# Three raw weight buffers of 1024 words in place of two of 1120, in a fp32 transformer kernel

## The chip, the cores and the metric

The kernel runs on one core of a Trainium2 chip. The metric is the device time of one execution in microseconds (us); smaller is better. A kernel's figure is the median of several executions.

## The reference

The input is one sequence of 512 tokens with 1024 features in fp32, and 256 memory tokens. Two blocks follow each other. Cut to what matters here:

```python
def first_block(x, mem, ...):
    for i in range(2):
        ...
        x = x + jnp.concatenate([y_tok, y_mem], axis=-1) @ w_out
        h = rmsnorm(x, norm_ffn[i])
        x = x + (jax.nn.silu(h @ w_gate[i]) * (h @ w_up[i])) @ w_down[i]
    return rmsnorm(x, final_norm)

def compress_blocks(kv, pe, w1, w2):
    ...
    flat = blocks.transpose(0, 2, 1, 3).reshape(n_cmp, G, CMP_LEN * dh)
    return jax.nn.gelu(flat @ w1) @ w2

def second_block(x, ...):
        h = rms_norm(x, norm_pre)
        proj = h @ w_in
        (q_n, k_c, v_c, k_s, v_s, k_w, v_w, g_n, z_n,
         q_r, k_r, v_r, z_r, m_a, m_b) = jnp.split(proj, split_points(), axis=-1)
        ...
```

In the first block `y_tok` is a short convolution (layer 0) or a banded attention of 128 tokens (layer 1), `y_mem` an attention to the memory tokens. The second block has sparse attention (compressed keys, selected keys and a window, mixed by gates), a retention with four heads, and a gated merge. Hidden width of the feed-forwards is 2816.

## The kernel before

All activations stay in SBUF, features on partitions and 512 tokens along the free dimension, so a row of 1024 features is eight chunks of 128 x 512. Nearly all time is matmuls on PE, and each fp32 product is made of three: operands are split into a high part (a copy to float32r) and a low part (the rest), and high by high, high by low and low by high are added in PSUM. Tiles named ...h and ...l are such pairs.

Weights pass through `weights` (L103). It takes a raw tile `wr` of 1120 words a partition, tag wr with 2 buffers; SP issues the load (L111), ACT copies it to the high part `wh` (L70), and DVE subtracts to get the low part `wl` (L80). Tags wh and wl have 3 buffers each, so a weight's products must be done before the third weight after it can be split. Most weight units are 1024 words. The token-major projection of the values and gates (`w_in_vg`, here vg) is 8 x 280 columns in two units of four, which makes 1120 words; it is the only one over 1024. Its products (L142 to L144) go to four PSUM banks, one for each block of 128 tokens, tags pp and lg in turn, and each runs over eight chunks: four of the first unit, four of the second.

The feed-forwards (`ffn`, L651) have 22 hidden groups f of 128 x 2 features in bundles. The first 5 are plain, the other 17 are made by a Strassen-like scheme with 7 products in place of 8 (`gate_up`, L593). For each f, `pair_weights` (L562) takes **two** raw tiles (L569), copies and splits them into wh and wl (the parts a22 and a11), splits a12, and makes four sums s1 to s4 on DVE (L582), each split again on ACT and DVE. In `gate_up` a product is 12 matmuls (L603 to L605). One bank of tag pp, U, collects a11, s2, s3 and a22 one after the other, and ACT copies its partial states to g1, g2 and u in between; products a12, s1 and s4 go to other banks, and DVE adds them to g and u (L610). Products s1 and s4 share a bank, so the s4 product starts when DVE's add on u has read it; silu (L627) and two multiplications follow. Between the products, `between` puts down-projections of the bundle before.

In `second` (L956) the row R is spread over the partitions (`spread`, L198), the first key and the first value are projected and scaled by R, then two further keys (each scaled to a tile f, rotated in rb and ra, and split into stacks kh and kl), then vg, then a query, a gate, and the compression of k (`compress`, L809): flat tiles get an added position table pe (L823), are split, and meet four weight units of `cmp_w1` in 48 short matmuls (L832 to L834). The compression of v follows with further gates between, then the attention heads (`causal_head`, L923), which add the table `causal` to their logits. The causal table and the rows are constants with a place of their own; slots are tiles of 512 words by tag, with a number of buffers for each tag (s has 3, t 4, sa 1, k3 2, v3 1).

Each engine runs its instructions in the order in which they stand in its queue. That order is not the one of the code: the framework's scheduler makes it at build time, from what it takes each instruction to last and from when buffers of a tag come free. A change of buffers therefore moves instructions on all engines.

Of the kernel before, what the change touches and what calls it, by code (L numbers as in the profile page):

```python
# [8 lines left out]
F32 = mybir.dt.float32  # L9
# [19 lines left out]
class Build:  # L29
# [5 lines left out]
    def __init__(self, ctx, tc, T, out):  # L35
        self.tc, self.nc, self.T, self.out = tc, tc.nc, T, out
        pool = lambda n, b, **k: ctx.enter_context(tc.tile_pool(name=n, bufs=b, **k))
        self.cst = pool("cst", 1)
        self.wp = pool("wp", 1)
        self.wbufs = dict(wr=2, wh=3, wl=3)  # L40
        self.sl = pool("sl", 1)
        self.sm = pool("sm", 4)
        self.psp = pool("psp", 1, space=PSUM)
        self.dr = pool("dr", 1, space=DRAM)
        self.n = 0
        self.bufs = dict(h=8, b=16, t=4, pa=6, pb=10, q=4, v=4, x=8, R=1, s=3, sa=1, k3=2, v3=1)
        self.pbufs = dict(pp=2, lg=3, tp=2, po=1)
# [55 lines left out]
    def weights(self, src, nk, nn, parts=1):  # L103

        nc, n = self.nc, nk * nn
        raw = self.wp.tile([128, 1120], F32, name=self.nm("wr"), tag="wr", bufs=self.wbufs["wr"])
        hi = self.wp.tile([128, WMAX], F32R, name=self.nm("wh"), tag="wh", bufs=self.wbufs["wh"])
        lo = self.wp.tile([128, WMAX], F32R, name=self.nm("wl"), tag="wl", bufs=self.wbufs["wl"])
        step = n // parts
        for s in (slice(a, a + step) for a in range(0, n, step)):  # L110
            nc.sync.dma_start(raw[:, s], src[:, s] if parts > 1 else src)  # L111
        for s in (slice(a, a + step) for a in range(0, n, step)):
            self.copy(hi[:, s], raw[:, s])
            self.lo_of(lo[:, s], raw[:, s], hi[:, s])
        v = lambda t: t[:, :n].rearrange("p (k c) -> p k c", k=nk)
        return v(hi), v(lo)

# [80 lines left out]
    def spread(self, rs, name):  # L198

        nc, nt = self.nc, rs.shape[1]  # L200
        dg = self.slot("s", name="dg")
        for t in range(nt):
            nc.vector.tensor_scalar(dg[:, t * 128:t * 128 + 128], self.ident, rs[:, t:t + 1], None, op0=ALU.mult)
        ps = self.psum("tp")
        n = nt * 128
        nc.tensor.matmul(ps[:, :n], self.ones, dg[:, :n], start=True, stop=True)
        r = self.const(name, [128, n]) if n < 512 else self.slot("R", name=name)
        self.copy(r, ps[:, :n])
        return r

# [84 lines left out]
    def load_consts(self):  # L295
        nc, T = self.nc, self.T
        self.ident = self.const("ident", [128, 128])
        self.gains = self.const("gains", [128, 8 * 8])
        self.const("pad", [128, 88])
        self.ones = self.const("ones", [128, 128])  # L300
        nc.vector.memset(self.ones, 1.0)
        self.zero = self.const("zero", [128, 128], F32R)
        self.copy(self.zero, self.ones, 0.0)
        nc.scalar.dma_start(self.gains, T["gains"])
        nc.scalar.dma_start(self.ident, T["ident"])
        self.x = [self.slot("x", name="x") for _ in range(8)]
        nc.sync.dma_start(self.x[0], T["x"][:, 0])
        self.h0 = self.gained(self.x[:1], self.gain(0))
        self.w0 = [self.weights(T["a_w_in"][i], 8, 128, 2) for i in (0, 12)]
        for c in range(1, 8):  # L310
            nc.sync.dma_start(self.x[c], T["x"][:, c])
        self.conv = self.const("conv", [128, 18])
        nc.scalar.dma_start(self.conv, T["conv"])
        self.sink = self.const("sink", [128, 12])
        nc.scalar.dma_start(self.sink, T["b_sinks"].to_broadcast([128, 12]))
        self.negsink = self.const("negsink", [128, 12])
        nc.vector.tensor_scalar(self.negsink, self.sink, -1.0, None, op0=ALU.mult)
# [244 lines left out]
    def pair_weights(self, src):  # L562


        nc = self.nc
        k = lambda t: t.rearrange("p (k c) -> p k c", k=4)
        raw = [self.wp.tile([128, 1120], F32, name=self.nm("wr"), tag="wr", bufs=self.wbufs["wr"])[:, :1024] for _ in range(2)]
        for i, r in enumerate(raw):
            nc.sync.dma_start(r, src[:, 1024 * i:1024 * i + 1024])  # L569
        a22, a11, a12, a21 = (r[:, u:u + 512] for r in raw for u in (0, 512))  # L570
# [238 lines left out]
    def compress(self, kT, j):  # L809

        nc, T = self.nc, self.T
        pe = self.small(32)
        nc.gpsimd.dma_start(pe, T["cmp_pe"][j])
        fl = [self.slot("pb", name="flat")[:, :496].rearrange("p (l c) -> p l c", l=8) for _ in range(2)]
        for half in range(2):
            for par in range(2):
                for g in range(2):
                    src = kT[64 * g:64 * g + 64]
                    first = 16 * half + par
                    a = src[:, first:first + 1]  # L820
# [6 lines left out]
        for u in range(4):  # L827
            wh, wl = self.weights(T["cmp_w1"][j, u], 4, 256)
            for k in range(4):
                i = 4 * u + k  # L830
                a, b = (f[:, 62 * (i % 8):62 * (i % 8) + 62] for f in fs[i // 8])
# [124 lines left out]
    def second(self):  # L956
        nc, T = self.nc, self.T
# [12 lines left out]
        R = self.spread(rs, "R2")  # L970
# [2 lines left out]
        self.xd = self.dr.tile([8, 128, 512], F32, name="xraw")  # L973
        for c in range(8):
            nc.gpsimd.dma_start(self.xd[c], self.x[c])
        self.causal = self.const("causal", [128, 512])
        nc.gpsimd.dma_start(self.causal, T["causal"])
        self.cmask = self.const("cmask", [128, 128])
        nc.gpsimd.dma_start(self.cmask, T["cmask"])
# [340 lines left out]
```

## Time and profile before

| | |
|---|---|
| median of 3 runs | 1644.36 us (1644.22 to 1647.47) |
| profiled execution | 1646.98 us |
| its span in the trace | 1645.2 us |
| mean granted clock of PE in it | 0.996 |
| weight loads of the pairs (in_w_gu) | 68 of 512 KB, 3.9 us from issue to landing |
| weight loads of vg | 2 of 560 KB, 3.8 us |

The profiled execution is one run with its own time; the span is what the trace covers of it. Times of single instructions come from this execution. Engines are PE (matmul; PEld is its weight load), DVE (VectorE), ACT (ScalarE), POOL (GpSimd) and SP (which issues DMAs). A row of a timeline gives start, duration, engine, line, operation and the tiles, out<-in; in brackets is the idle time of that engine just before and what ended it. Instructions of PE overlap, so its pace is the distance between starts.

### The profile page before, as it was taken

The page shows a single profiled execution, that of the slowest core. Times are in us where ns is not written, and L with a number is a line of the kernel's source. Part 1 is how long each engine was busy: PE and PEld are TensorE (multiplying, and loading weights), DVE is VectorE, ACT ScalarE, POOL GpSimd, SP SyncE. Part 2 cuts the span into 40 slices and gives each one's busy share as a digit, 9 for nine tenths or more (in the row PEclk, how much of TensorE's full clock was granted, in tenths as well). Part 3 has the DMA queues.
Part 4 walks back from the last instruction along what each step waited for, and adds up shares of the span by engine and source line. Part 5 has one row for each costly group of instructions (what it writes and reads, how often), then busy time and mean ns, then how long its engine had stood idle before and what let it go on. Part 6 is the DMA issues. An engine that isn't in the chain of part 4 may idle for free.

```text
span 1645.2 us, 24463 instructions
## 1 busy us (share of the span) xinstructions
PE 1610.8 (98%) x9408; PEld 1408.5 (86%) x9408; DVE 1236.5 (75%) x2335; ACT 761.0 (46%) x1410; POOL 170.2 (10%) x179
## 2 busy tenths in 40 slices
PE   8999999999999999999999999998999999999998
PEld 6887888999999888888889999987888888888888
DVE  7876778777776889878777777698788877764444
ACT  6633344444444567625444444445465533333333
POOL 1112410000000300041000000111000000010011
PEclk9999999999999999999999999999999999999999
DMA  6227322333333623132332332343501122243342
GB/s 204 92 90 202 106 90 91 103 111 96 113 97 97 200 70 97 53 115 77 103 103 88 106 103 96 110 143 100 164 26 59 46 84 84 71 154 116 127 160 90
DMA packets 53877, 174.23 MB, mean 106 GB/s; under 512 B 6936, under 2 KB 9184, under 8 KB 53632
## 3 DMA queue, kind: packets, MB, share of 16 engines
q1 hardware_dynamic: 44928, 150.06, 28.0%
q0 software_dynamic: 8256, 22.49, 4.3%
q8 instruction: 74, 1.21, 0.3%
q14 instruction: 43, 0.35, 0.1%
q10 hardware_dynamic: 576, 0.11, 0.0%
HBM read 161.35 MB, written 13.65 MB: 106 GB/s over the span
## 4 chain that ended last, share of the span: by engine, by line
PE 75%; DVE 12%; DMA 6%; ACT 3%; issue 3%; POOL 1%; SPq 0%; DVEq 0%; ACTq 0%; POOLq 0%
PE pp L121 8%; PE pp L120 8%; PE pp L122 8%; DMA wr<-in_w_gu_dram 4%; PE lg L120 4%; PE lg L121 3%; PE lg L122 3%; DVE wl L80 3%; PE pp L603 3%; PE pp L604 3%; PE pp L605 3%; PE tp L120 3%; PE tp L121 3%; PE tp L122 3%; PE tp L262 2%
## 5 line engine op out<-in xcount | busy, mean ns | idle before, releaser
L70 ACT ACTIVATE wh<-wr 128x1024 fp32r<-128x1024 f32 (+3 forms) x246 | 252.0, 1024 | 344.8 <-PE pp L121 141.0
L80 DVE TENSOR_TENSOR wl<-wr,wh 128x1024 fp32r<-128x1024 f32 (+3 forms) x246 | 306.8, 1248 | 52.6 <-ACT wh L70 51.4
L120 PE MATMUL pp<-g,wh 128*128 128x512 f32 x592 | 235.0, 397 | 8.1 <-ACT wh L70 7.2
L122 PE MATMUL pp<-g,wl 128*128 128x512 f32 x592 | 234.4, 396 | 0.9 <-DVE wl L80 0.9
L121 PE MATMUL pp<-g,wh 128*128 128x512 f32 x592 | 233.1, 394 | 0.0
L120 PEld LDWEIGHTS pp<-g,wh 128*128 128x128 f32 x592 | 111.9, 189 | 31.0 <-ACT wh L70 8.2
L122 PEld LDWEIGHTS pp<-g,wl 128*128 128x128 f32 x592 | 111.6, 189 | 23.6 <-DVE wl L80 2.7
L121 PEld LDWEIGHTS pp<-g,wh 128*128 128x128 f32 x592 | 111.8, 189 | 20.3 <-DVE g L76 0.3
L70 ACT ACTIVATE s<-s 128x512 fp32r<-128x512 f32 x136 | 85.2, 631 | 52.1 <-DVE s L582 49.8
L120 PE MATMUL tp<-acth,wh 128*128 128x512 f32 x264 | 103.3, 391 | 0.0
L121 PE MATMUL tp<-actl,wh 128*128 128x512 f32 x264 | 103.3, 391 | 0.0
L122 PE MATMUL tp<-acth,wl 128*128 128x512 f32 x264 | 102.8, 389 | 0.0
L80 DVE TENSOR_TENSOR s<-s,s 128x512 fp32r<-128x512 f32 x136 | 90.3, 685 | 0.0
L603 PE MATMUL pp<-Bh,s 128*128 128x256 f32 x272 | 78.2, 288 | 3.3 <-ACT g L70 3.0
L582 DVE TENSOR_TENSOR s<-wr,wr 128x512 f32<-128x512 f32 x68 | 46.8, 689 | 44.6 <-DMA wr<-in_w_gu_dram 44.4
L603 PE MATMUL lg<-Bh,s 128*128 128x256 f32 x272 | 77.7, 286 | 0.8 <-DVE u L610 0.8
L605 PE MATMUL lg<-Bh,s 128*128 128x256 f32 x272 | 77.2, 284 | 0.0
L605 PE MATMUL pp<-Bh,s 128*128 128x256 f32 x272 | 76.9, 283 | 0.0
L248 POOL MEMSET v<- 128x1152 f32 x8 | 8.3, 1062 | 541.0 <-PE lg L605 541.0
L627 ACT ACTIVATE g<-g 128x512 f32<-128x512 f32 x34 | 21.5, 632 | 88.0 <-DVE g L610 88.0
L122 PEld LDWEIGHTS tp<-acth,wl 128*128 128x128 f32 x264 | 49.6, 188 | 10.9 <-DVE wl L80 0.3
L610 DVE TENSOR_TENSOR g<-lg,g 128x256 f32<-128x256 f32 x68 | 28.8, 423 | 38.8 <-PE lg L605 38.8
(512 smaller groups left out, 4611.5 us busy)
## 6 DMA issues: line engine op xcount, KB each, us to landing
wr<-in_w_gu_dram SPq DMA_DIRECT2D x68, 512.0 KB, 3.9
wr<-in_w_in_dram SPq DMA_DIRECT2D x44, 512.0 KB, 3.5
wr<-in_w_down_dram SPq DMA_DIRECT2D x32, 512.0 KB, 3.7
wr<-in_a_w_in_dram SPq DMA_DIRECT2D x18, 512.0 KB, 3.5
wr<-in_w_down_dram SPq DMA_DIRECT2D x16, 384.0 KB, 3.2
wr<-in_w_gate_dram SPq DMA_DIRECT2D x10, 512.0 KB, 3.5
wr<-in_w_up_dram SPq DMA_DIRECT2D x10, 512.0 KB, 3.5
wr<-in_a_w_out_dram SPq DMA_DIRECT2D x8, 512.0 KB, 3.5
```

The source lines that it names most:

```text
L70: self.nc.scalar.activation(out, in_, AF.Copy, scale=scale)
L80: self.nc.vector.tensor_tensor(out, x, hi.bitcast(F32), op=ALU.subtract)
L120: mm(ps, ah, bh, start=start, stop=False)
L121: mm(ps, ah, bl, start=False, stop=False)
L122: mm(ps, al, bh, start=False, stop=stop)
L262: self.nc.tensor.transpose(ps[:, c:c + 128], src, self.ident)
L582: nc.vector.tensor_tensor(t, a, b, op=ALU.add)
L603: mm(ps, ah, bh, start=start and j == 0, stop=False, skip_group_check=not start)
L604: mm(ps, ah, bl, start=False, stop=False, skip_group_check=not start)
L605: mm(ps, al, bh, start=False, stop=j == 3, skip_group_check=not start)
L610: add = lambda out, a, b: nc.vector.tensor_tensor(out, a, b, op=ALU.add)
L627: nc.scalar.activation(g, g, AF.Silu)
```

## The change

Raw tiles get three buffers of 1024 words in place of two of 1120. A vg unit is loaded in two pieces: 1024 words into the raw tile and 96 words into a slot of tag s, each with a load, a copy to the high part and a subtraction of its own. To make room, the causal table moves from a constant to a slot of tag sa, the memory row R of 256 tokens to a slot of tag v3, the position table of the compression to a slot of tag k3, and a padding constant shrinks from 88 words to 24.

```diff
-        self.wbufs = dict(wr=2, wh=3, wl=3)
+        self.wbufs = dict(wr=3, wh=3, wl=3)
...
-        raw = self.wp.tile([128, 1120], F32, name=self.nm("wr"), tag="wr", bufs=self.wbufs["wr"])
+        raw = self.wp.tile([128, 1024], F32, name=self.nm("wr"), tag="wr", bufs=self.wbufs["wr"])
...
-        step = n // parts
-        for s in (slice(a, a + step) for a in range(0, n, step)):
-            nc.sync.dma_start(raw[:, s], src[:, s] if parts > 1 else src)
-        for s in (slice(a, a + step) for a in range(0, n, step)):
-            self.copy(hi[:, s], raw[:, s])
-            self.lo_of(lo[:, s], raw[:, s], hi[:, s])
+        m = min(n, 1024)
+        step = m // parts
+        pieces = [(slice(a, a + step), raw[:, a:a + step]) for a in range(0, m, step)]
+        if n > m:
+            pieces.append((slice(m, n), self.slot("s", name="wr")[:, :n - m]))
+        for s, r in pieces:
+            nc.sync.dma_start(r, src if len(pieces) == 1 else src[:, s])
+        for s, r in pieces:
+            self.copy(hi[:, s], r)
+            self.lo_of(lo[:, s], r, hi[:, s])
...
-        r = self.const(name, [128, n]) if n < 512 else self.slot("R", name=name)
+        r = self.slot("v3", F32, (128, 576), name)[:, :n] if n < 512 else self.slot("R", name=name)
...
-        self.const("pad", [128, 88])
+        self.const("pad", [128, 24])
...
-        raw = [self.wp.tile([128, 1120], F32, name=self.nm("wr"), tag="wr", bufs=self.wbufs["wr"])[:, :1024] for _ in range(2)]
+        raw = [self.wp.tile([128, 1024], F32, name=self.nm("wr"), tag="wr", bufs=self.wbufs["wr"]) for _ in range(2)]
...
-        pe = self.small(32)
+        pe = self.slot("k3", F32, (128, 128), "pe")[:, :32]
...
-        self.causal = self.const("causal", [128, 512])
+        self.causal = self.slot("sa", name="causal")
```

The order of PE's instructions stays but for the first products of each feed-forward and the stretch of `second` from R to the end of the attention. Below are two places, on two engines each. Behind `weights` the changed kernel's lines are numbered 4 higher (its load is L115).

**The start of the first feed-forward.** ACT around the copies from U (pp_2501) of the first f before; wr_2639 is the second half of the second pair, wr_2793 of the third, and s_... are the sums:

```order
L70 ACTIVATE a_513_2646<-wr_2639 128x512
L70 ACTIVATE s_515_2651<-s_514_2649 128x512
L70 ACTIVATE g_2504<-pp_2501 128x256
L70 ACTIVATE s_517_2656<-s_516_2654 128x512
L70 ACTIVATE s_519_2661<-s_518_2659 128x512
L70 ACTIVATE s_521_2666<-s_520_2664 128x512
L70 ACTIVATE u_2505<-pp_2501 128x256
L627 ACTIVATE g_2504<-g_2504 128x512
```

and in the changed kernel:

```order
L70 ACTIVATE g_2504<-pp_2501 128x256
L70 ACTIVATE s_518_2656<-s_517_2654 128x512
L70 ACTIVATE s_520_2661<-s_519_2659 128x512
L70 ACTIVATE g_2504<-pp_2501 128x256
L70 ACTIVATE s_522_2666<-s_521_2664 128x512
L70 ACTIVATE a_539_2800<-wr_2793 128x512
L70 ACTIVATE u_2505<-pp_2501 128x256
L70 ACTIVATE s_541_2805<-s_540_2803 128x512
L70 ACTIVATE s_543_2810<-s_542_2808 128x512
L70 ACTIVATE wh_2766<-wr_2765 128x1024
L631 ACTIVATE g_2504<-g_2504 128x512
```

The copies of the third pair's a12 (from wr_2793) and of two of its sums now stand ahead of silu, the first one ahead of the copy to u_2505.

DVE ahead of the add on u of the second f (u_2673) before, where the data are the third pair's (wr_2792, wr_2793):

```order
L80 TENSOR_TENSOR wl_2797<-wr_2792,wh_2796 128x1024
L610 TENSOR_TENSOR g_2672<-lg_2670,g_2672 128x256
L582 TENSOR_TENSOR s_539_2803<-wr_2793,wr_2792 128x512
L80 TENSOR_TENSOR a_538_2800<-wr_2793,a_538_2800 128x512
L582 TENSOR_TENSOR s_541_2808<-s_539_2803,wr_2792 128x512
L80 TENSOR_TENSOR s_540_2805<-s_539_2803,s_540_2805 128x512
L582 TENSOR_TENSOR s_543_2813<-wr_2792,wr_2793 128x512
L80 TENSOR_TENSOR s_542_2810<-s_541_2808,s_542_2810 128x512
L582 TENSOR_TENSOR s_545_2818<-s_541_2808,wr_2793 128x512
L610 TENSOR_TENSOR u_2673<-lg_2671,u_2673 128x256
```

and in the changed kernel, where wr_2940 and wr_2941 are the fourth pair:

```order
L80 TENSOR_TENSOR wl_2797<-wr_2792,wh_2796 128x1024
L80 TENSOR_TENSOR actl_2635<-act_2631,acth_2634 128x512
L614 TENSOR_TENSOR g_2672<-lg_2670,g_2672 128x256
L80 TENSOR_TENSOR s_545_2815<-s_544_2813,s_545_2815 128x512
L586 TENSOR_TENSOR s_562_2951<-wr_2941,wr_2940 128x512
L586 TENSOR_TENSOR s_564_2956<-s_562_2951,wr_2940 128x512
L80 TENSOR_TENSOR s_547_2820<-s_546_2818,s_547_2820 128x512
L586 TENSOR_TENSOR s_566_2961<-wr_2940,wr_2941 128x512
L80 TENSOR_TENSOR a_561_2948<-wr_2941,a_561_2948 128x512
L614 TENSOR_TENSOR u_2673<-lg_2671,u_2673 128x256
```

Ahead of that add stand now four steps that need the fourth pair, all of which wait for its second half, and the third pair's sums have moved forward.

**The values of `second`.** SP's loads around vg before:

```order
L111 DMA wr_11277<-in_w_in_vg_dram 128x1120
L111 DMA wr_11283<-in_w_in_vg_dram 128x1120
L111 DMA wr_11421<-in_w_in_dram 128x1024
L111 DMA wr_11461<-in_w_in_dram 128x1024
L111 DMA wr_11517<-in_cmp_w_dram 128x1024
L111 DMA wr_11535<-in_cmp_w_dram 128x1024
L111 DMA wr_11553<-in_cmp_w_dram 128x1024
L111 DMA wr_11571<-in_cmp_w_dram 128x1024
```

and in the changed kernel, where wr_11280 and wr_11290 are the two pieces of 96 words:

```order
L115 DMA wr_11277<-in_w_in_vg_dram 128x1024
L115 DMA wr_11287<-in_w_in_vg_dram 128x1024
L115 DMA wr_11429<-in_w_in_dram 128x1024
L115 DMA wr_11469<-in_w_in_dram 128x1024
L115 DMA wr_11525<-in_cmp_w_dram 128x1024
L115 DMA wr_11280<-in_w_in_vg_dram 128x96
L115 DMA wr_11543<-in_cmp_w_dram 128x1024
L115 DMA wr_11290<-in_w_in_vg_dram 128x96
L115 DMA wr_11561<-in_cmp_w_dram 128x1024
L115 DMA wr_11579<-in_cmp_w_dram 128x1024
```

Each piece stands behind one weight unit of the compression. DVE from the row's scale to the third f (f_11256) before, where wl_11279 and wl_11285 are vg's low parts:

```order
L73 TENSOR_TENSOR f_11133<-pp_11102,R_2029_11061 128x512
L475 COPY rs_11081<-rz_11077 128x4
L73 TENSOR_TENSOR v_c_11141<-pp_11142,R_2029_11061 128x512
L788 STREAM_SHUFFLE rb_11136<-f_11133 128x512
L80 TENSOR_TENSOR wl_11279<-wr_11277,wh_11278 128x1120
L73 TENSOR_TENSOR rb_11136<-rb_11136,nrope_11100 128x512
L793 TENSOR_TENSOR ra_11135<-ra_11135,rb_11136 128x512
L823 TENSOR_TENSOR flat_11498<-ra_11135,m_11496 64x8x31 x4
L823 TENSOR_TENSOR flat_11499<-ra_11135,m_11496 64x8x31 x2
L73 TENSOR_TENSOR f_11205<-pp_11174,R_2029_11061 128x512
```

and in the changed kernel, from the low part of vg's first unit (wl_11279) on:

```order
L80 TENSOR_TENSOR wl_11279<-wr_11277,wh_11278 128x1024
L73 TENSOR_TENSOR f_11133<-pp_11102,R_2030_11061 128x512
L73 TENSOR_TENSOR v_c_11141<-pp_11142,R_2030_11061 128x512
L792 STREAM_SHUFFLE rb_11136<-f_11133 128x512
L73 TENSOR_TENSOR rb_11136<-rb_11136,nrope_11100 128x512
L797 TENSOR_TENSOR ra_11135<-ra_11135,rb_11136 128x512
L827 TENSOR_TENSOR flat_11506<-ra_11135,pe_11504 64x8x31 x4
L827 TENSOR_TENSOR flat_11507<-ra_11135,pe_11504 64x8x31 x4
L80 TENSOR_TENSOR fll_11517<-flat_11506,flh_11516 128x496
L73 TENSOR_TENSOR f_11205<-pp_11174,R_2030_11061 128x512
L80 TENSOR_TENSOR fll_11521<-flat_11507,flh_11520 128x496
```

The low part stands now ahead of the first f (f_11133), and all eight additions to the flat tiles ahead of the second (f_11205). Behind that one, and ahead of the third, come additions for the compression of v (flat_11638) in the changed kernel:

```order
L792 STREAM_SHUFFLE rb_11208<-f_11205 128x512
L80 TENSOR_TENSOR wl_11289<-wr_11287,wh_11288 128x1024
L73 TENSOR_TENSOR rb_11208<-rb_11208,nrope_11100 128x512
L827 TENSOR_TENSOR flat_11638<-v_c_11141,pe_11636 64x8x31
L797 TENSOR_TENSOR ra_11207<-ra_11207,rb_11208 128x512
L827 TENSOR_TENSOR flat_11638<-v_c_11141,pe_11636 64x8x31 x3
L233 TENSOR_TENSOR kl_11214<-ra_11207,kh_11213 64x512 x2
L233 TENSOR_TENSOR kl_11220<-ra_11207,kh_11219 64x512 x2
L73 TENSOR_TENSOR f_11256<-pp_11225,R_2030_11061 128x512
```

which the kernel before has behind the third f.

## Rows read from the trace of the kernel before

**Rows 1.** The page, part 1: busy time, share of the span and instructions of each engine.
```profile
PE 1610.8 (98%) x9408; PEld 1408.5 (86%) x9408; DVE 1236.5 (75%) x2335; ACT 761.0 (46%) x1410; POOL 170.2 (10%) x179
```

**Rows 2.** The table of waits of PE: waiter, releaser, then us in total, times, longest us.
```profile
PE pp L603 <- ACT u L70: 3.9, 4, 1.3
PE pp L603 <- ACT g L70: 3.0, 7, 0.7
PE pp L832 <- ACT wh L70: 2.4, 1, 2.4
PE pp L834 <- DVE wl L80: 1.5, 2, 0.9
```

**Rows 3.** The page, part 5: ACT's copies of raw weights, with what ended ACT's idle time.
```profile
L70 ACT ACTIVATE wh<-wr 128x1024 fp32r<-128x1024 f32 (+3 forms) x246 | 252.0, 1024 | 344.8 <-PE pp L121 141.0
```

**Rows 4.** Timeline of SP's issues, 255 to 320: start us, us, instruction.
```profile
275.49 2.78 SPq L569 DMA_DIRECT2D wr<-in_w_gu_dram  x2
286.99 15.61 SPq L569 DMA_DIRECT2D wr<-in_w_gu_dram  x4
```

**Rows 5.** Timeline of ACT, 262 to 312; in brackets the idle time before and its releaser.
```profile
282.56 0.63 ACT L70 ACTIVATE a<-wr 128x512 fp32r<-128x512 f32 x1 [2.15 <-DMA wr<-in_w_gu_dram]
287.56 0.37 ACT L70 ACTIVATE u<-pp 128x256 f32<-128x256 f32 x1
```

**Rows 6.** Timeline of DVE, 262 to 312.
```profile
288.65 0.42 DVE L610 TENSOR_TENSOR u<-lg,u 128x256 f32<-128x256 f32 x1
295.28 1.22 DVE L80 TENSOR_TENSOR wl<-wr,wh 128x1024 fp32r<-128x1024 f32 x1
302.12 0.42 DVE L610 TENSOR_TENSOR u<-lg,u 128x256 f32<-128x256 f32 x1
```

**Rows 7.** DMA issues: tile, queue, count, KB of each, median us from issue to landing.
```profile
wr<-in_w_gu_dram SPq DMA_DIRECT2D x68, 512.0 KB, 3.9
s<-in_onehot_dram POOLq DMA_DIRECT2D x1, 48.0 KB, 2.8
```

**Rows 8.** Timeline of DVE at the start of the second feed-forward.
```profile
809.96 0.42 DVE L610 TENSOR_TENSOR u<-lg,u 128x256 f32<-128x256 f32 x1
826.41 0.42 DVE L610 TENSOR_TENSOR u<-lg,u 128x256 f32<-128x256 f32 x1
```

**Rows 9.** Windows: busy us (instructions) of PE, PEld, DVE, ACT, POOL, then PEclk, DMA share, GB/s.
```profile
811.00:814.60 3.60, 3.60 (x19) 3.59 (x18) 0.46 (x2) 0.94 (x2) 0.00 (x0) 0.53 0.23 93
1142.70:1149.00 6.30, 5.42 (x24) 5.03 (x25) 2.73 (x3) 2.83 (x4) 0.00 (x0) 0.50 0.57 192
1149.00:1190.00 41.00, 40.19 (x207) 33.01 (x207) 31.79 (x77) 19.92 (x36) 1.97 (x2) 1.00 0.51 164
1190.00:1300.00 110.00, 108.35 (x623) 90.17 (x622) 99.27 (x292) 70.83 (x194) 6.28 (x6) 1.00 0.10 33
```

**Rows 10.** Timeline of ACT, 1097 to 1152.
```profile
1099.72 0.60 ACT L70 ACTIVATE R<-tp 128x512 f32<-128x512 f32 x1 [2.55 <-PE tp L206]
1100.48 1.14 ACT L70 ACTIVATE wh<-wr 128x1120 fp32r<-128x1120 f32 x1 [0.15 <-PE pp L121]
```

**Rows 11.** Timeline of DVE, 1095 to 1152.
```profile
1105.05 3.59 DVE L823 TENSOR_TENSOR flat<-ra,m 64x248 f32<-64x248 f32 x6
1115.29 2.78 DVE L229 TENSOR_TENSOR kl<-ra,kh 64x512 fp32r<-64x512 f32 x4
1118.10 0.69 DVE L73 TENSOR_TENSOR f<-pp,R 128x512 f32<-128x512 f32 x1
```

**Rows 12.** Timeline of PE, 1107.8 to 1115.3: end of the key projections, start of vg.
```profile
1107.83 0.39 PE L122 MATMUL pp<-g,wl 128*128 128x512 f32 x1
1112.13 0.29 PE L142 MATMUL pp<-wh,g 128*128 128x280 f32 x1
1115.23 0.29 PE L142 MATMUL lg<-wh,g 128*128 128x280 f32 x1
```

**Rows 13.** Timeline of PE in the compression of k.
```profile
1142.70 0.47 PE L832 MATMUL pp<-wh,flh 128*62 128x256 f32 x1 [2.40 <-ACT wh L70]
```

## The prediction

> **What bounds the kernel now.** I read the page's busy shares first, then the table of waits of TensorE (PE), then the stretches where those waits stand. PE is busy 98% of the span, VectorE (DVE) 75% and ScalarE (ACT) 46% [rows 1], so a change can win only what PE loses by waiting, and can lose a lot by making PE wait. The waits that end with weights are short: the feed-forward products wait 3.9 and 3.0 us in all for ACT's copies of u and g, the compression 2.4 us for a high part and 1.5 us for a low part [rows 2]. Behind ACT's copies of raw weights stands mostly not the DMA: of the 344.8 us that ACT idles before them, 141.0 are ended by PE, which gives back a buffer of high parts, tag wh [rows 3]. A third raw buffer doesn't move that. So the raw buffers bind only at the start of each feed-forward and in the compression, and elsewhere I take the change to be worth nothing.
>
> **The start of the first feed-forward.** A pair takes two raw buffers. With two in all, the second pair is issued from 275.49 on and the third from 286.99 on [rows 4], and ACT waits for the second pair 2.15 us before its part a12 and copies u at 287.56 [rows 5]. With three, the second pair's last half no longer waits behind the down weight, so it goes about 2.7 us earlier, at 275.5, and lands 3.9 us later [rows 7], at 279.4. That is a gain, but the order then spends it: ACT now has the third pair's a12 ahead of u, and DVE has two operations of the third pair ahead of the add on u. The third pair's second half must wait until DVE has finished the sums of the second. From 279.4 on DVE has eight steps of about 0.6 us there and one low part of 1.22, one held to 280.9 by a down product: it is through at about 285.6, the half lands at 289.5, ACT copies a12 in 0.63, DVE does two steps, and the add on u ends at 291.2. Now it starts at 288.65 and takes 0.42 [rows 6], so this is 2.1 us later, and the s4 product on PE waits for it.
>
> For the next f the same stands in the order with the fourth pair, and five DVE steps ahead of the add, four of them on that pair's data. Its second half needs the buffer that the low part at 295.28 gives back [rows 6]. That low part stands behind silu and the two products of act, so with 2.1 us of delay and the steps between I get its end at 298.0, the landing at 301.9, five steps to 305.2, and the add done at 305.6, where it is done at 302.54 now. From there on PE is continuously fed and the delay is simply carried: **+3.1 us**. Bounds: if the low part keeps its present end of 296.5, +1.6; if the landing is as slow as 0.7 us more, +3.8; if the earlier second pair were all that counts, half of the 6.9 us of [rows 2] would go, -3.5. I take +3.1, since the order names each step.
>
> **The start of the second feed-forward** has the same order. There the two adds on u stand at 809.96 and 826.41 [rows 8], 16.5 us apart against 13.5 in the first, because PE already loses time there: its clock is 0.53 for 3.6 us [rows 9], some 1.7 us of loss. The second add's start by my walk, 305.2, moved by the distance between the two first adds, 521.3, is 826.5: no later than now. **0 us**, from -1.7 (a clock that does not fall) to +3.1.
>
> **The token values (vg), in `second`.** A unit of 1120 words becomes 1024 plus 96. The two extra loads of 48 KB cost SP's queue two places. The nearest rows for one are 2.8 us for 48 KB and 3.9 us for 512 KB [rows 7]; I take 2.8. What counts is what they wait for: each sits in a slot of tag s, and by the order the first is issued only when the second key copy of the first stack is done with it, the second when the rotation of the second stack is. Behind the first one on SP stand compression weights, which have a buffer early enough. ACT and DVE get two more copies and two more low parts of 96 words, some 0.3 us each; on DVE they stand in the middle of a chain that PE waits for.
>
> The walk: ACT makes the row R at 1099.72 and the high part of vg 0.76 later [rows 10]; the order swaps them, R ends 1.8 us later, and DVE has vg's low part ahead of the first f. f therefore starts 2.4 us later. Up to the third f, at 1118.10, DVE gets four additions for the compression of v more, of 0.6 us each (six take 3.59) [rows 11], and has that low part of 1.34 behind it already: 2.4 + 2.4 - 1.3 = +3.5, so the third f ends at 1122.2. PE starts vg at 1112.13 now, and 24 of its products go by in 3.10 us, 0.129 each; the 19 of 512 columns before them took 4.30 us, 0.226 each [rows 12]. It now ends the key projections 2.1 us later, at 1114.3, has 17 of vg's products to do, and then needs the bank that the third f empties: idle from 1116.5 to 1122.2, 5.7 us. After 13 more products it needs the first 96-word low part, eight DVE steps behind that f (one of 1.22), at 1127.4: 3.5 us idle. After 16 more it needs the second, behind one addition and four low key parts of 2.78 together [rows 11], at 1131.1: 1.6 us idle. The last 36 take 4.6, so vg ends at about 1135.7 where it ends at 1125.1 now: **+10 us**, at least +3.5 if DVE keeps its present times.
>
> Most of this comes back. While PE waits, the compression weights load into the free third buffer, and ACT and DVE split them. The 2.4 and 1.5 us of waits go; the fall of the clock to 0.50 for 24 matmuls that follows the 2.40 us of idle time [rows 13] goes too, and is worth half of 5.42 us, 2.7 [rows 9]: **-6.6**. From 1149 to 1190, 207 matmuls take 41 us [rows 9]; five products of 24 at 0.226, 48 short ones at half of 5.42 / 24 = 0.113, and the other 39 at vg's 0.129 make 37.6. Weights that are there early save most of the rest, **-3**, from 0 to -3.4. The 22 causal logits that now partly fill this stretch move behind it; that is time moved, not won. Net **+0.4**.
>
> **The clock.** An idle stretch of 2.40 us is followed by 6.3 us at 0.50 [rows 9, 13]. 5.7 us and 3.5 us of waiting in vg should do the same, and part of the slow matmuls stand beside further waits: **+2**, between 0 and twice the 2.7 above.
>
> **The attention behind it.** From 1190 to 1300 DVE is busy 99.27 of 110 us [rows 9]. The softmax work that goes with those logits now falls into this stretch, which is a little full already: **+1**, from 0 to +4. The causal table, the memory row and the position table are in slots that become free long before they are needed; their loads are on POOL's queue, whose waits PE does not share: 0.
>
> **The sum**: 3.1 + 0 + 0.4 + 2 + 1 = 6.5 us on the profiled execution's 1646.98, 1653.5. That execution lies 2.6 us above the median of 1644.36 (a span of 1645.2 and 1.8 us around it), so for the median I forecast 1644.36 + 6.5 = **1650.9 us**.
>
> **The rivals.**
> *The buffer does what it is for.* DVE has more slack in vg than my walk gives it, so only the 3.5 us of the lower bound is lost there, the compression gives its 6.6 and 3 back, and the feed-forwards lose nothing: 3.5 - 6.6 - 3 = -6.1, **1638.3 us**. It decides if the third f ends within about 1 us of its present time. For it: the waits on weights are real [rows 2], and the loads do start earlier. Against it: the order puts more DVE work ahead of that f. The Trainium skill (Perfetto Trace Analysis, Optimization Strategy) reads a gap that keeps repeating on the engine that should be saturated as a sign of too few buffers; by it this rival would be the likeliest. The trace bears it out only in part: PE's waits for u and g number 4 and 7 in 34 gate-up blocks [rows 2]. Chance 0.20.
>
> *No change.* The wh buffers hold the weights back [rows 3], the later order at the feed-forward start eats just the earlier load, and vg gains and loses alike: **1644 to 1647 us**. Chance 0.25.
>
> *The clock falls at every longer wait.* In the first feed-forward the two waits grow from about 2 us to 3 and more, and the second shows that 0.53 can follow there [rows 9]: 1.7 us more for each of the two feed-forwards and 2.7 more in vg, 6.5 + 6.1, **1657.0 us**. The Trainium skill (TensorE: Matmul & The Clock Gate, What's actually happening) lets the clock depend on how busy PE has been recently; by it this rival follows from the forecast's waits. The trace agrees at 2.40 us of idle time, but not at the first feed-forward's start, where no fall is seen. Chance 0.13.
>
> **How the numbers follow.** The forecast has the rest, 0.42. 0.2%, 3.3 us, is about what a measurement of this kernel can tell from no change. The forecast and the clock rival are slower but for some 0.02 of the forecast: 0.53 slower, 0.25 + 0.02 = 0.27 same, 0.20 faster. The range takes in the no-change case, the clock rival with its 1657.0 and 2 us more, and the first rival's upper half: 1639 to 1659. The slower cases alone would have 1648 to 1659.
>
> **What would show it.** In the changed profile: the adds on u in the first feed-forward near 290.8 and 305.2, ended by the DMA of the pair; PE idle 4 to 6 us before the third vg block, released by DVE's f, and twice more by the 96-word low parts; no wait in the compression of k; a stretch of clock 0.5 near 1125; from 1300 on the same rows as now, shifted. I am wrong if the third f starts before 1120, if the fourth pair lands before 300, or if the compression still waits for wh.

## The result and the profile after

The changed kernel is slower: 1655.63 us in the median (1653.11 to 1657.51, 4 runs) against 1645.09 for the kernel before in the same comparison. The ratio is 1.0060, with a 95% interval of 1.0048 to 1.0072. The forecast of 1650.9 had the sign right and the range too, which is wide (1639 to 1659, with no change in it), but only 6.5 of the 10.5 us.

The page, part 1, and the waits of PE of the changed kernel (waiter, releaser, us in total, times, longest us), which answer to [rows 1] and [rows 2]; the last block has two waits of the kernel before that [rows 2] leaves out:

```profile
PE 1615.1 (98%) x9408; PEld 1412.4 (85%) x9408; DVE 1237.7 (75%) x2337; ACT 759.0 (46%) x1412; POOL 170.0 (10%) x179
```

```profile
PE pp L607 <- ACT u L70: 6.2, 2, 3.4
PE pp L146 <- DVE f L73: 5.2, 1, 5.2
PE lg L607 <- DVE u L614: 3.6, 4, 2.2
PE pp L607 <- ACT g L70: 3.1, 6, 0.8
PE pp L148 <- DVE wl L80: 2.0, 1, 2.0
...
PE pp L838 <- DVE wl L80: 1.2, 2, 1.0
PE lg L148 <- DVE wl L80: 0.5, 1, 0.5
```

```profile
PE lg L603 <- DVE u L610: 0.8, 2, 0.4
...
PE pp L142 <- DVE f L73: 0.4, 1, 0.4
```

The waits for u have grown from 3.9 to 6.2 us (longest 3.4) and those for the add on it from 0.8 to 3.6 (longest 2.2). The wait for the third f has grown from 0.4 to 5.2 us, and 2.0 and 0.5 us for low parts in vg (L148) are new. Of these the 2.0 us are for the first piece of 96 words. The 0.5 us are not for a piece: they stand at 1109.66, where PE meets the low part of the first 1024 words, and no wait for the second piece is seen. The 2.4 us for a high part in the compression are gone; of the 1.5 us for low parts there 1.2 are left. The first feed-forward's start, SP, ACT and DVE, answering to [rows 4 to 6]:

```profile
273.18 0.90 SPq L573 DMA_DIRECT2D wr<-in_w_gu_dram  x2
...
283.78 13.26 SPq L573 DMA_DIRECT2D wr<-in_w_gu_dram  x4
```

```profile
289.00 0.63 ACT L70 ACTIVATE a<-wr 128x512 fp32r<-128x512 f32 x1 [3.75 <-DMA wr<-in_w_gu_dram]
289.54 0.37 ACT L70 ACTIVATE u<-pp 128x256 f32<-128x256 f32 x1
```

```profile
289.04 0.69 DVE L586 TENSOR_TENSOR s<-wr,wr 128x512 f32<-128x512 f32 x1 [2.31 <-DMA wr<-in_w_gu_dram]
289.67 0.69 DVE L80 TENSOR_TENSOR a<-wr,a 128x512 fp32r<-128x512 f32 x1
290.27 0.42 DVE L614 TENSOR_TENSOR u<-lg,u 128x256 f32<-128x256 f32 x1
...
301.25 0.69 DVE L586 TENSOR_TENSOR s<-wr,wr 128x512 f32<-128x512 f32 x1 [0.25 <-DMA wr<-in_w_gu_dram]
...
304.65 0.42 DVE L614 TENSOR_TENSOR u<-lg,u 128x256 f32<-128x256 f32 x1
```

ACT stands 3.75 us at the a12 of the third pair, and u, which PE had ready, is copied behind it. The loads themselves are earlier than before: both halves of the second pair go out within 0.90 us of 273.18, where they took 2.78 from 275.49 on.

The same kind of row stands in a place that the prediction didn't name, late in the second feed-forward. DVE, 940 to 942:

```profile
940.76 0.69 DVE L586 TENSOR_TENSOR s<-wr,wr 128x512 f32<-128x512 f32 x1 [4.35 <-DMA wr<-in_w_gu_dram]
941.37 0.41 DVE L614 TENSOR_TENSOR u<-lg,u 128x256 f32<-128x256 f32 x1
```

And PE behind it:

```profile
941.84 0.39 PE L607 MATMUL lg<-Bh,s 128*128 128x256 f32 x1 [2.19 <-DVE u L614]
```

DVE has nothing to do for 4.35 us, because the first sum of a pair still on its way stands ahead of the add on u; PE gets that add 2.19 us late. PE's clock in four stretches behind such waits follows (windows, columns as in [rows 9]). Each clock is a mean over its window, which mixes the two levels 1.00 and 0.50:

```profile
290.00:294.00 4.00, 4.00 (x23) 4.00 (x24) 2.98 (x7) 0.90 (x2) 0.00 (x0) 0.64 0.01 4
816.00:820.00 4.00, 4.00 (x24) 4.00 (x23) 3.03 (x6) 0.77 (x3) 0.00 (x0) 0.60 0.00 0
942.00:948.00 6.00, 6.00 (x32) 5.70 (x33) 5.23 (x10) 2.75 (x5) 0.00 (x0) 0.72 0.00 0
1126.00:1138.00 12.00, 6.98 (x29) 6.65 (x30) 11.67 (x21) 5.38 (x10) 2.19 (x1) 0.57 0.17 52
```

And vg, on DVE (answering to [rows 11]), on SP, and what SP waited for ahead of the two pieces; the last block has the loads' time from issue to landing (answering to [rows 7]):

```profile
1123.65 1.73 DVE L827 TENSOR_TENSOR flat<-v_c,pe 64x248 f32<-64x248 f32 x3
1125.41 2.78 DVE L233 TENSOR_TENSOR kl<-ra,kh 64x512 fp32r<-64x512 f32 x4
1128.23 0.69 DVE L73 TENSOR_TENSOR f<-pp,R 128x512 f32<-128x512 f32 x1
...
1134.11 0.26 DVE L80 TENSOR_TENSOR wl<-wr,wh 128x96 fp32r<-128x96 f32 x1
...
1137.82 0.26 DVE L80 TENSOR_TENSOR wl<-wr,wh 128x96 fp32r<-128x96 f32 x1
```

```profile
1128.40 0.33 SPq L115 DMA_DIRECT2D wr<-in_w_in_vg_dram  x1
...
1133.50 0.33 SPq L115 DMA_DIRECT2D wr<-in_w_in_vg_dram  x1
```

```profile
SPq L115 <- DVE kl L233: 5.9, 1, 5.9
SPq L115 <- DVE ra L797: 3.0, 1, 3.0
```

```profile
wr<-in_w_gu_dram SPq DMA_DIRECT2D x68, 512.0 KB, 3.9
...
wr<-in_w_in_vg_dram SPq DMA_DIRECT2D x2, 48.0 KB, 1.8
```

The third f starts at 1128.23, behind four additions for v (three in the row shown) and four low key parts. The 96-word pieces are issued only at 1128.40 and 1133.50, after SP has waited for DVE's low key parts kl (5.9 us) and rotation ra (3.0 us), the uses of their slots that the prediction names.

Where the time went is read from starts of the same matmul in two traces, since PE's order is the same at these places. Each column is a difference of two profiled executions, in us gained or lost within the stage; the first two are two pairs of executions of the same two kernels. The last column sets the kernel with the order held (below) against the changed kernel's second execution; the two ran on two chips, on which the kernel before has medians of 1645.48 and 1645.97:

| stage | change less before | again | order held less changed kernel |
|---|---|---|---|
| up to 260 us | +0.4 | -0.5 | +0.7 |
| first feed-forward, start | +1.7 | +1.3 | -3.5 |
| first feed-forward, later | +1.3 | +1.5 | -1.6 |
| up to the second one | 0.0 | -0.1 | +0.1 |
| second feed-forward, start | -0.8 | +2.9 | -4.8 |
| second feed-forward, later | +4.9 | +2.3 | -1.4 |
| up to vg | +0.3 | -0.4 | +0.1 |
| vg, compression, attention | +3.2 | +3.1 | +0.3 |
| from there to the last matmuls | -0.2 | +0.2 | 0.0 |
| sum | +10.7 | +10.4 | -10.1 |

### The profile page after: what moved, and what is told of

It is laid out like the page before. It is cut to its first block, busy times and chain, and to the rows that moved or that the text cites. A ratio compares the mean times of both kernels' runs of the same rounds, so it can differ in the third digit from the quotient of the medians.

```text
span 1655.7 us, 24513 instructions
## 1 busy us (share of the span) xinstructions
PE 1615.1 (98%) x9408; PEld 1412.4 (85%) x9408; DVE 1237.7 (75%) x2337; ACT 759.0 (46%) x1412; POOL 170.0 (10%) x179
## 4 chain that ended last, share of the span: by engine, by line
PE 78%; DVE 11%; DMA 6%; ACT 2%; issue 2%; POOL 1%; DVEq 0%; SPq 0%; ACTq 0%; POOLq 0%
PE pp L125 8%; PE pp L126 8%; PE pp L124 8%; DMA wr<-in_w_gu_dram 5%; PE lg L124 4%; PE lg L125 4%; PE lg L126 4%; PE pp L607 3%; PE pp L609 3%; PE pp L608 3%; PE tp L124 3%; PE tp L125 3%; PE tp L126 3%; PE tp L266 2%; PE lg L607 2%; DVE wl L80 2%
## 5 line engine op out<-in xcount | busy, mean ns | idle before, releaser
L70 ACT ACTIVATE wh<-wr 128x1024 fp32r<-128x1024 f32 (+3 forms) x248 | 251.9, 1016 | 327.8 <-PE pp L125 130.7
L80 DVE TENSOR_TENSOR s<-s,s 128x512 fp32r<-128x512 f32 x136 | 93.8, 701 | 13.5 <-ACT s L70 13.1
L673 DVE TENSOR_TENSOR x<-x,tp 128x512 f32<-128x512 f32 x72 | 49.0, 681 | 15.4 <-PE tp L126 15.3
L126 PEld LDWEIGHTS tp<-acth,wl 128*128 128x128 f32 x264 | 49.6, 188 | 10.7
L607 PEld LDWEIGHTS lg<-Bh,s 128*128 128x128 f32 x272 | 52.8, 194 | 6.5 <-DVE u L614 5.3
```

The source lines that it names most:

```text
L70: self.nc.scalar.activation(out, in_, AF.Copy, scale=scale)
L80: self.nc.vector.tensor_tensor(out, x, hi.bitcast(F32), op=ALU.subtract)
L126: mm(ps, al, bh, start=False, stop=stop)
L607: mm(ps, ah, bh, start=start and j == 0, stop=False, skip_group_check=not start)
L673: nc.vector.tensor_tensor(x, x, ps, op=ALU.subtract)
```

## The experiments

The theory is that the order makes the loss: with a third raw buffer the scheduler puts steps of the pair after next ahead of u, and vg's work in another order, and in-order engines then stand at loads that aren't there. Rivals: the pieces and their slots do it; or the buffer itself, by its crowding loads.

**Two raw buffers, all else as changed.**

```diff
-        self.wbufs = dict(wr=3, wh=3, wl=3)
+        self.wbufs = dict(wr=2, wh=3, wl=3)
```

> The whole change but for the third raw buffer: two raw buffers of 1024 words, vg's pieces of 96 words in slots of tag s, the tables in slots. The changed kernel's profile is 10.5 us above that of before. Order theory: about 7 us of it are feed-forward steps of the pair after next that the third buffer lets the scheduler put ahead of the add on u; without it each pair stands one ahead of u again, so the feed-forwards are as before, and only the two waits for the pieces in vg remain, with no compression weights loaded early to pay for them: +2 to +5 us on before, 1647 to 1650. Pieces theory (the pieces and their slots carry most of it): +6 to +10, 1651 to 1655. Buffer theory (the third buffer's loads crowd the DMA queues, the order is harmless): 0 to +1, 1645 to 1646.

Measured: 1646.84 us, ratio 1.0012 (1.0001 to 1.0023). Nearly all of the loss goes with the third buffer; the pieces theory falls as the main cause. The time lies just under the 1647 of the order theory and above the 1646 of the buffer theory, so order and loads are not told apart by it. By its profile the feed-forwards stand 0.7 us better than in the kernel before (its second execution, below) and vg to attention 2.0 us worse, as the order theory has it.

**vg's pieces in tiles of their own, three buffers.**

```diff
-            pieces.append((slice(m, n), self.slot("s", name="wr")[:, :n - m]))
+            pieces.append((slice(m, n), self.wp.tile([128, 96], F32, name=self.nm("wx"), tag="wx", bufs=2)[:, :n - m]))
```

> The whole change, but vg's two pieces of 96 words have two small tiles of their own in place of slots of tag s, and are loaded near the program's start (a padding constant is 8 words smaller). Order theory: the feed-forwards keep their 7 us; in vg the waits for the two low parts (2.0 and 0.5 us in the changed profile) go, the wait of 5.2 us for the third f stays in part: 1655.6 less 2 to 4, 1651.5 to 1653.5. Pieces theory: most of the 10.5 us go, 1645 to 1648. Buffer theory: no change against the changed kernel, 1655 to 1656.

Measured: 1651.05, 1.0043 (1.0028 to 1.0058), just under what the order theory has: the feed-forwards keep their loss, and its profile has 1.9 us of wait for the third f in place of 5.2 and none of 2.0 for a low part. The third f itself comes hardly sooner (it starts 18.4 us behind the first f, in the changed kernel 18.7). But with the pieces there, PE's order has 50 of vg's 96 products ahead of the bank that this f empties, in place of 27, so most of the 5.2 us, too, was owed to the late pieces. Vg to attention turns from a loss of 3.1 to 3.2 us into a gain of 2.3 on the kernel before. By this stage own tiles are worth some 5 us with three buffers; by the medians only 0.8 to 2.8 (1.0043 against 1.0048 and 1.0060). Its later part of the second feed-forward lost 3.9 us in the profiled execution, where the changed kernel lost 4.9 and 2.3; that may hide a part, and the rest of the difference is left open.

**The slot moves alone** (causal table, memory row and position table, in the kernel before; the edits are those lines of the change).

> The kernel before with the moves of the tables alone: causal table, memory row and position table in slots; raw buffers and vg as before. All theories: within 1 us of before, 1644 to 1646, since PE never waits for these tables. A rise of 2 us or more would say that the moves count.

Measured: 1646.59, 1.0013 (1.0001 to 1.0024). That is 0.2 to 3.9 us: a small rise is likely, and one of 2 us is neither shown nor excluded. Its profile has no loss behind 260 us against the kernel before (its second execution), so no place of it is known.

**The order held in the feed-forwards.** The weights of a pair are queued behind the copy and the add on u of two blocks earlier; it is an order of issue on ACT and DVE only:

```diff
-        nc, w = self.nc, self.pair_weights(src)
+        nc = self.nc
+        if first:
+            self.held = []
+        with ExitStack() as st:
+            for ins in (self.held[-2] if len(self.held) > 1 else []):
+                st.enter_context(self.tc.issue_after(ins))
+            w = self.pair_weights(src)
...
-        self.copy(u, U)
-        add(u, Z, u)
+        cu = nc.scalar.activation(u, U, AF.Copy, scale=1.0)
+        au = add(u, Z, u)
+        self.held.append((cu.ins, au.ins))
```

> The whole change, with one order held by hand: in the feed-forwards the copies, sums and low parts of the pair after next stay behind the copy and the add on u of the present f on ACT and DVE, so that one pair stands ahead of u as before; loads, buffers and vg stay as in the changed kernel. Order theory: the 7 us in the feed-forwards go (waits for u and the two falls of the clock there), 1655.6 less 6 to 8, 1647.5 to 1649.5. Buffer theory and pieces theory: as the changed kernel, 1654 to 1657.

Measured: 1643.34, 0.9988 (0.9978 to 0.9999). The changed kernel stands at 1.0060 and, in a later comparison, at 1.0048, each against the kernel before on its own chip, so the order alone is worth 0.6 to 0.7%, 10 to 12 us. Loads and buffers stand in the program as they did, so the buffer theory falls. ACT and DVE of this kernel at the first feed-forward's start:

```profile
286.34 0.38 ACT L631 ACTIVATE u<-pp 128x256 f32<-128x256 f32 x1 [1.26 <-PE pp L615]
289.33 0.63 ACT L70 ACTIVATE a<-wr 128x512 fp32r<-128x512 f32 x1 [2.60 <-DMA wr<-in_w_gu_dram]
```

```profile
286.76 0.42 DVE L620 TENSOR_TENSOR u<-lg,u 128x256 f32<-128x256 f32 x1 [0.21 <-ACT u L631]
...
300.96 0.42 DVE L620 TENSOR_TENSOR u<-lg,u 128x256 f32<-128x256 f32 x1 [0.84 <-ACT u L631]
```

The a12 of the third pair is copied at 289.33 as before its move (289.00), but u, at 286.34, no longer waits for it. The adds stand at 286.76 and 300.96, where the kernel before has 288.65 and 302.12 [rows 6]: the earlier loads are worth 1 to 2 us once nothing is queued behind them. I had expected -6 to -8 us; it is -10 to -12, and this gain, on top of the loss that goes, is a part of the difference.

**Both repairs**: own tiles and held order.

> Three raw buffers, vg's pieces in small tiles of their own and loaded near the start, and one pair ahead of u held in the feed-forwards. Order theory: the two repairs add, since they lie in different stages: held order alone stands at 0.9988 of before (some -2 us, with vg still 2.9 us worse by its profile), and the own tiles turn vg's +2.9 into -2.7 by theirs, so -2 - 5.6 = some -7.5 us on before, 1637 to 1639.5, ratio 0.994 to 0.997. Buffer theory: a third buffer is worth nothing once its harm is gone, ratio 1.000 with at most 0.1% either way.

Measured: 1640.37, 0.9970 (0.9960 to 0.9981); again in a later comparison, 1640.83, 0.9975 (0.9965 to 0.9985). It beats both kernels, by 4 to 5 us on the one before. That is less than the 7.5 expected: own tiles add 2 to 3 us to the held order and not 5.6, and the profiles have vg to attention at -2.1 and -1.0 and the feed-forwards at -1.4 and -2.8, against before.

**Order held in the first feed-forward only**, pieces in slots:

```diff
-            for ins in (self.held[-2] if len(self.held) > 1 else []):
+            for ins in (self.held[-2] if len(self.held) > 1 and self.layer == 0 else []):
...
+        self.layer = layer
```

> The changed kernel with the order held in the first feed-forward only; pieces in slots of tag s as in the change. Order theory, by the profiles: held order wins 3.7 + 1.7 us in the first feed-forward and 9 in the second, falls of the clock included; so some -4 to -5.5 us on the changed kernel's ratio of 1.0060, 1.0027 to 1.0037, and 1.0060 - 0.9988 less that is left in the second. Rival (a global effect of the loads, not of single waits): either nothing, or all of it.

Measured: 1649.82, 1.0033 (1.0019 to 1.0047), within what was expected: the loss belongs to single places, and with one half of them held about half of it is left. In its profile the first feed-forward gains 2.6 us on before, and the second loses 7.0.

**Two buffers, pieces in tiles of their own.**

> Two raw buffers of 1024 words, with vg's pieces in small tiles of their own. Order theory: the feed-forwards are as before, vg loses its waits for the pieces, and the compression waits for its weights as before: within 1.5 us of before, and 1 to 3 us less than two buffers with the pieces in slots (1.0012). If instead it wins 3 us or more on before, the gain in vg is the pieces' early load and not the third buffer's.

Measured: 1647.52, 1.0017 (1.0007 to 1.0026). No gain on the kernel before: own tiles win in the medians only with three buffers. That it is not better than two buffers with slots (1.0012) was not expected. In the profiles own tiles do help at their place: vg to attention loses 0.5 us on the kernel before (its second execution), against 2.0 with slots. But this execution had lost 4.1 us before 260 us, where the other lost 1.0; whether that belongs to the kernel is left open, and the two intervals overlap.

**The third f ahead of the additions for v**, on top of both repairs:

```diff
+        self.third = self.f_last.ins
...
-                pv = self.compress(v_c, 1)
+                with self.tc.issue_after(self.third):
+                    pv = self.compress(v_c, 1)
```

> As the kernel with both repairs, and DVE's additions for the compression of v are held behind the third f of the key projections. Order theory: the 2.05 us for which PE waits for that f in the own-tiles kernel shrink to under 0.5, less what the additions then cost later: -0.5 to -1.5 us on the kernel with both repairs. Rival: DVE is full in this stretch (busy nearly all of 1100 to 1134), so moving three additions of 0.6 us only moves the wait to the compression: 0 to +1.

Measured: 1642.79, 0.9985 (0.9975 to 0.9996), slower than both repairs. PE's waits in the two kernels, first this one, then both repairs:

```profile
PE pp L843 <- ACT wh L70: 2.4, 1, 2.4
PE pp L845 <- DVE wl L80: 2.2, 3, 1.0
...
PE pp L146 <- DVE f L1004: 0.9, 1, 0.9
```

```profile
PE pp L146 <- DVE f L73: 1.9, 1, 1.9
PE pp L845 <- DVE wl L80: 1.6, 2, 1.1
...
PE pp L843 <- ACT wh L70: 0.6, 1, 0.6
```

The wait for f falls from 1.9 to 0.9, and those of the compression rise from 2.2 to 4.6. A second execution of both repairs has 3.5 there, so a part of that rise is scatter. DVE is nearly full here (32.59 of 34 us from 1100 to 1134), and its work comes due at the next place. The expectation fell, and its rival, 0 to +1 us, has the right sign: the loss is 2.4 us in the medians, and 2.6 and 1.5 us from vg to attention against the two executions of both repairs.

**Vg's weights behind R and the first f**, on top of both repairs:

```diff
+        row = self.r_copy.ins
...
+        first = self.f_last.ins
...
-        self.proj_tok(T["w_in_vg"], h, 280, 4, done, tag=("pp", "lg"))
+        with self.tc.issue_after(row), self.tc.issue_after(first):
+            self.proj_tok(T["w_in_vg"], h, 280, 4, done, tag=("pp", "lg"))
```

> The kernel with both repairs, and vg's weights held behind the row R on ACT and behind the first f on DVE, as they stand before the change. Prediction's step: in the changed order the third f starts some 2.4 us later for R and the low part alone; here the 2.04 us for which PE waits for that f go to 0.5, PE loses nothing for it, and the time is 1 to 2 us less than with both repairs (0.997), 0.9955 to 0.9965. Rival: the time only moves to the compression, where DVE's low parts are late again: 0.997 to 0.9985.

> The kernel with both repairs once more, for the comparison on one chip with the one above: 0.996 to 0.998 of before.

Measured on one chip: 1640.93, 0.9976 (0.9965 to 0.9987), against 0.9975 (0.9965 to 0.9985). The same. PE's waits from 1070 to 1300, first of this kernel, then of both repairs:

```profile
PE pp L843 <- ACT wh L70: 2.4, 1, 2.4
PE pp L845 <- DVE wl L80: 2.0, 3, 1.1
PE pp L124 <- DVE f L1005: 1.4, 1, 1.4
```

```profile
PE pp L843 <- ACT wh L70: 2.1, 1, 2.1
PE pp L146 <- DVE f L73: 1.9, 1, 1.9
PE pp L845 <- DVE wl L80: 1.4, 2, 1.1
```

The wait of 1.9 us for the third f goes, and 1.4 us for an earlier f, in the projections ahead of vg, and 0.9 us more in the compression stand in its place. So the rival's time held, but only a part of the wait moved to the compression, where it had put all.

**The kernels before and after once more.**

> The kernel before, unchanged, as a measure of scatter. In its first profile PE's clock fell at the start of the second feed-forward; in three later kernels with the same order there it did not, and they gained some 4 us at that place. Those kernels also all stood 0.9 to 1.5 us or more behind it by 50 us. If both are scatter: ratio 1.000 with 0.1%, and this profile shows either no fall there or a start as late as theirs, or both. If the slot moves cost something of their own: its start is again 1 us or more ahead of theirs, and the ratio is 0.998 to 0.999 of theirs.

> The changed kernel, unchanged, on the chip of the experiments. Order theory: its waits for u and the third f stand in every run, so the ratio is 1.005 to 1.007 again, and this profile has PE's waits for u near 290 and 815 of 2.5 us or more and one for f of some 5 us. The falls of the clock may differ: if one of those in the first profile is missing, the time is 2 to 4 us less than with it.

Measured: before 1644.98, 0.9997 (0.9986 to 1.0007); changed 1654.26, 1.0048 (1.0033 to 1.0063). The start of this profile of before is 0.5 us later than that of the first, and its clock falls at the start of the first feed-forward and not of the second. The second profile of the changed kernel has the waits that were expected, 5.4 us for u (longest 2.8) and 5.2 for the third f, and lacks the fall at 942 to 948 (1.00 in place of 0.72). Windows of PE in the kernel before, first profile, then this one (us, busy us, clock, DMA share, GB/s):

```profile
808.00:816.00 8.00, 6.30 (x31) 0.79 0.38 131
288.00:296.00 8.00, 7.59 (x53) 1.00 0.40 144
```

```profile
808.00:816.00 8.00, 6.26 (x42) 1.00 0.38 131
288.00:296.00 8.00, 7.59 (x41) 0.79 0.32 126
```

## Why the prediction was right in sign and short in size

**The first feed-forward's start**, +3.1: the mechanism is the one in the rows, ACT at the third pair's a12. The add was to end at 291.2 and ends at 290.69; the next one was to start at 305.2 and starts at 304.65. The stage lost only 1.7 and 1.3 us, though PE's clock fell to 0.64 behind the wait, which the forecast had not put here. The second pair went out at 273.18 and not at 275.5, and PE made good a part of the delay. The term is of the right kind and about twice too large.

**The second one's start**, 0: -0.8 in one pair of executions and +2.9 in the other. The difference lies in the clock of the kernel before, which fell there in the first pair only, and my term was made against that execution. Against the execution without it the stage loses 2.9.

**"From there on PE is continuously fed"**, and the statement that elsewhere the change is worth nothing, are the steps that failed. The order has the first sum of the pair after next ahead of the add on u in two more blocks of each feed-forward (near 413 and 428, 941 and 958), and the prediction leaves them out without a reason. The stages with them lose 1.3 and 1.5 us in the first feed-forward, and 4.9 and 2.3 in the second, with a fall of the clock in the dearer execution (0.72 at 942 to 948) and none in the other. Together they lose 6.2 and 3.8 us that the forecast put at nothing. With the two starts (-2.2 and +1.1 us against the forecast) and small differences elsewhere, this makes the some 4 us by which the forecast was short. The load time was not the matter: the pairs land in 3.9 us as before [rows 7].

**Vg**, +10, has the right places, and its net is right in part by luck. Vg's last matmul starts at 1143.06 for 1125.00, 18.1 us later, of which 7.7 were carried in, so 10.4 are vg's. PE waits 5.2 us for the third f (5.7 in my walk), then 2.0 for the first piece (3.5) and nothing for the second (1.6): 7.2 us in place of 10.8. The pieces took 1.8 us to land, for which I had taken 2.8. (The walk also counts 92 of vg's 96 products, with the 10 that the order puts ahead, some 0.5 us.) The fall of the clock makes up for it: 6.98 us of matmuls at 0.57 are, as an estimate, 3.0 us lost within vg, where the forecast has 2 beside the 10. And 7.2 us came back by the end of the attention, not 6.6 + 3 - 1 = 8.6. The net is +3.2 and +3.1, where 0.4 + 2 + 1 = 3.4 had been forecast. The experiments put a cause under it: with own tiles the stretch is better than before by 2.3 us (2.1 and 1.0 with held order), so the slots' late release costs here and not the third buffer.

**The rival that the buffer does what it is for** was false for the change as it was made and true for the mechanism: held to one pair, the loads are a gain of 1 to 2 us at the starts, and with the pieces repaired the kernel is at 0.997. **The clock rival**, 1657.0, lies nearer to the result than the forecast, by luck: it has 3.1 + 1.7 us for the first start, which lost 1.7 and 1.3, and nothing for the later blocks. The clock did fall at both starts and in vg, to 0.64, 0.60 and 0.57 in the windows shown; in the first two alone that is, as an estimate, 4 x 0.36 + 4 x 0.40 = 3.0 us of lost clock. But the kernel before has such falls too (1.7 us at 0.53 [rows 9]), and held order removes waits and falls together, so the changed kernel's falls are not priced by themselves. The two executions of the kernel before give two prices: they part by 3.3 us at the second start, where only the first has the fall, and by 0.2 us in the end at the first start, where only the second has it. The Trainium skill's sentence that the clock follows how busy PE has been recently (TensorE: Matmul & The Clock Gate, What's actually happening) agrees with these rows, though it cannot say in which of two executions a wait of 1.3 us is followed by a fall.

**No change** was to hold because the wh buffers hold the weights back. They still do for the most part: ACT's idle time for its copies went from 344.8 to 327.8 us, of which PE ends 130.7 in place of 141.0 [rows 3]. This rival fell because the loss comes from the order, which it took to cancel out.

## What to carry to other kernels

Another buffer changes the order that a scheduler makes, and on in-order engines a step that waits for a load takes with it all that stands behind it (here ACT stood for 3.75 us and DVE for 4.35): after adding one, look in the new order for steps of later loads that have moved ahead of what the bounding engine waits for, and hold those. When such a row is found at one place, look for it in every repetition of the loop, also where the loop has work between. And a small piece that is put into a shared slot is as late as the slot's last user; give it its own room if PE will wait for it.

## What was not expected of the hardware

The same kernel, with the same order, has PE's clock at 0.79 in 808 to 816 in one execution and 1.00 in another, and the other way round at 288 to 296, with the same waits ahead: PE waits 1.34 us for u at either place in the first execution and 1.33 us in the second. This moves the second feed-forward's start by some 3 us, and may be a part of why single executions of the kernel before lie between 1640.98 and 1649.75 us. A term that rests on one profiled execution's clock carries that scatter.
